# Seven half-size products in place of eight in an encoder's gated MLP

## The chip, the cores and the metric

The kernel runs on one core of one Trainium2 chip. The metric is the device time of one execution in microseconds (us), the median of three runs. Nothing of the arithmetic is done on the host; the host only lays the arrays out.

## The reference

Two layers of an encoder on 512 tokens of 1024 features, float32. Each layer mixes tokens (neighbourhood attention beside a gated linear recurrence) and then goes through a gated MLP; `x` is added to after each of the two. What matters here is the MLP:

```
h = rmsnorm(x, g_ffn[l])
u = h @ w_up[l]                                   # 1024 -> 2 x 3072
u_act, u_lin = jnp.split(u, 2, axis=-1)
u_act = depthwise_conv(u_act, conv_ffn_w[l], conv_ffn_b[l], (1, 1))
x = x + (jax.nn.gelu(u_act, approximate=True) * u_lin) @ w_down[l]
```

`rmsnorm` divides each token by its root mean square over the features and multiplies by a gain per feature. The convolution has width 3 over neighbouring tokens.

## The kernel before

Features lie on the 128 partitions, tokens along the free axis: `x` is eight tiles `x[k]` of 128 x 512. A weight matrix is cut into blocks of 128 x 128. A matrix product in float32 is done as three products of a rounded type: each operand is split into a high part (a copy rounded to `fp32r`, on ACT) and a low part (what is left, a subtraction on DVE), and `mm3` (L242) multiplies high by high, high by low and low by high into one PSUM bank. So each 128 x 128 block of weights against 512 tokens is three matmuls of 512 columns.

Weights arrive in chunks of eight blocks (128 x 1024) in the order of `weight_plan` (L57). `chunk` (L231) takes the next one; before that it has the chunks up to three ahead split (`split_to`, L190: ACT at L205, DVE at L206) and those up to six ahead loaded by SP's DMA queue (`load_to`, L170, into the two buffers of `p_raw`). Some chunks of layer 1 are split during layer 0 (`split_later`, L212, one per call, 20 in all) by POOL's DMA queue and kept in DRAM. Tile buffers come from pools with a fixed count (`p_t` 12, `p_h` 24, `p_hi` and `p_lo` 4 each); an operation that wants a buffer waits until its last user is done. The order on each engine is fixed when the kernel is built: by priority in the order of the program, with `urgent` pieces moved forward.

The MLP of a layer begins with `x` times its gain, split (`scaled_split`); the token's factor `rbf` (one over the root mean square, the same for all features) is applied after the first product, since it commutes with it. It comes from the sum of squares over the features: a matmul with ones (`columns`, L394), a power on POOL (L399), transposes (L406) and a copy (L408). The 3072 hidden features are 24 tiles `j`; each has an activation tile (block column `j` of `w_up`) and a linear tile (block column 24 + `j`), called a pair here. Pairs 0 and 1 are computed together in four PSUM banks (`gemm_group`, tile name `up`); then each `j` takes 24 matmuls for `pa` and 24 for `pl`. `mlp_tile` (L843) does the rest of a pair: `ua = pa * rbf`, the convolution in three DVE operations, Gelu on ACT, the product with `pl`, and the split of the result into `hs[j]`.

After 12 pairs (HALF) their contribution to `w_down` is computed (`dn`): four output tiles in a group of four banks, then four one after another; `summed` (L882) multiplies by `rbf` where needed and adds to `x[m]`. Two halves make a layer. At the end of the last layer `finish` (L435) does the last two output tiles in two halves of 256 tokens, so that the final norm of the first half runs beside the products of the second; `probs_of`, the attention's probability buffers (L305), serve as output buffers there.

Tokens are stored in an order that groups them by eight columns of the grid; `natural` and `by_row` are views of a tile in the order of the convolution and back.

Of the kernel before, what the change touches and what calls it, by code (L numbers as in the profile page):

```python
# [14 lines left out]
P = 128  # L15
D = 1024
# [12 lines left out]
HALF = NJ // 2  # L29
# [26 lines left out]

def weight_plan():  # L57

    plan = []
    for l in range(L):  # L60
        def pairs(w, k0, nk, ms):
            for k in range(k0, k0 + nk, 2):
                plan.append((w, l, [(k + a, m) for a in range(2) for m in ms]))

        def column(w, m):
            plan.append((w, l, [(k, m) for k in range(8)]))

        pairs("w_in", 0, 8, [12, 13, 14, 15])
        for step in MIX:
            if step[0] == "V" and int(step[1]) % 2 == 0:  # L70
                pairs("w_in", int(step[1]), 2, [8, 9, 10, 11])
            elif step[0] == "t" and step[-1] != "b":
                plan.append(("gate", l, [(int(step[1]), dg) for dg in range(4)]))
            elif step[0] in IN_TILE and step[-1] != "b":
                column("w_in", IN_TILE[step[0]] + int(step[1]))
        for m in range(0, 8, 2):
            plan.append(("w_out", l, [(a, m + b) for b in range(2) for a in range(4)]))
        pairs("w_out", 4, 4, [0, 1, 2, 3])
        for m in (4, 6):
            plan.append(("w_out", l, [(4 + a, m + b) for b in range(2) for a in range(4)]))  # L80
        for hf in range(2):
            j0 = hf * HALF
            for j in range(j0, j0 + HALF):
                if j == 0:
                    pairs("w_up", 0, 8, [0, NJ, 1, NJ + 1])
                elif j > 1:
                    column("w_up", j)
                    column("w_up", NJ + j)
            pairs("w_down", j0, HALF, [0, 1, 2, 3])
            seq = [(j0 + k, m) for m in range(4, 8) for k in range(HALF)]  # L90
            for i in range(0, len(seq), 8):
                plan.append(("w_down", l, seq[i:i + 8]))
    return plan
# [15 lines left out]
def encoder(ctx: ExitStack, tc: tile.TileContext, x_d, w_d, cols_d, bias_d, out_d):  # L109
    nc = tc.nc  # L110
    plan = weight_plan()
# [14 lines left out]
    p_raw = pool("p_raw", 2)  # L126
# [28 lines left out]
    raws, highs, lows, halves, kept = {}, {}, {}, {}, {}  # L155
# [14 lines left out]
    def load_to(n):  # L170
        while state["load"] < min(n, len(plan)):
            i = state["load"]
            if is_kept(i):
                if i > state["use"] + 3:
# [8 lines left out]
            raws[i] = p_raw.tile([P, 1024], F32, tag="raw", name=f"raw{i}")  # L183
            for n, sl in enumerate(pieces(i)):
                nc.sync.dma_start(raws[i][:, sl], w_d[i][:, sl])
                if i == n == 0:
                    nc.sync.dma_start(x[0], x_d[0])
            state["load"] += 1

    def split_to(n):  # L190
        while state["split"] < min(n, len(plan)):
            i = state["split"]
# [796 lines left out]
```

## Time and profile before

| | |
|---|---|
| median of 3 runs | 1204.91 us (1204.35 to 1204.92) |
| the profiled execution's own time | 1204.35 us |
| its span, first to last instruction | 1202.6 us |
| PE busy, matmuls | 1188.4 us, 5534 |
| DVE busy | 752.9 us |
| ACT busy | 511.7 us |
| POOL busy | 114.0 us |
| granted TensorE clock, mean | 0.996 of full |

Busy time is the union of an engine's instructions. PE's matmuls are pipelined: one lasts 0.39 us in the records while the next begins 0.23 later, so the distance between starts is what one costs. The same holds in small for DVE and ACT. L with a number is a line of the kernel; since the helper `mm3` issues the matmuls, all of them stand at L243 to L245 and are told apart by the names of their tiles.

### The profile page before, as it was taken

The numbers are of one execution on the slowest core, as the hardware profiler recorded it, in microseconds if no ns is written. First come the engines' busy times: TensorE is split into PE (matmuls) and PEld (weight loads), VectorE is DVE, ScalarE is ACT, GpSimd is POOL, SyncE is SP. The second block draws the span as 40 slices with busy tenths as digits, with TensorE's granted clock in tenths as the row PEclk, the third lists the DMA queues.
The fourth block names the chain that finished last, engine by engine and source line by source line (L and its number), as shares of the span: only waits on it lengthen the run. The fifth ranks groups of instructions, "written<-read, shape, count | busy, mean of one in ns | idle before, by whom it ended". The sixth has DMA issues, their size and how long they took to land.

```text
span 1202.6 us, 14575 instructions
## 1 busy us (share of the span) xinstructions
PE 1188.4 (99%) x5534; PEld 992.1 (83%) x5534; DVE 752.9 (63%) x1226; ACT 511.7 (43%) x753; POOL 114.0 (9%) x230
## 2 busy tenths in 40 slices
PE   9999999999999999999999999999999999999996
PEld 8878888888888888888888888888888888888886
DVE  7988967776644567653736679587555336565443
ACT  6668854434321334422408578354233213333231
POOL 1102110123210122200002012000000000000000
PEclk9999999999999999999999999999999999999998
DMA  7222214376643376733256442232323232323222
GB/s 237 82 87 89 82 38 139 106 237 236 221 164 103 134 231 215 237 115 104 88 176 200 130 159 71 62 112 90 98 96 104 90 105 88 104 89 105 88 70 70
DMA packets 51046, 151.86 MB, mean 126 GB/s; under 512 B 6432, under 2 KB 9632, under 8 KB 50976
## 3 DMA queue, kind: packets, MB, share of 16 engines
q1 hardware_dynamic: 41792, 122.21, 31.1%
q0 software_dynamic: 8640, 28.32, 7.2%
q8 instruction: 43, 0.70, 0.2%
q10 hardware_dynamic: 544, 0.40, 0.1%
q14 instruction: 27, 0.22, 0.1%
HBM read 129.93 MB, written 20.97 MB: 125 GB/s over the span
## 4 chain that ended last, share of the span: by engine, by line
PE 91%; ACT 4%; DVE 3%; issue 1%; DVEq 0%; POOLq 0%; POOL 0%; ACTq 0%
PE dn L243 7%; PE dn L245 7%; PE dn L244 7%; PE pl L243 7%; PE pa L243 7%; PE pa L244 7%; PE pl L244 7%; PE pa L245 7%; PE pl L245 7%; PE out L245 2%; PE out L243 2%; PE out L244 2%; PE s L690 1%; PE xr L243 1%; PE up L243 1%; PE xr L244 1%
## 5 line engine op out<-in xcount | busy, mean ns | idle before, releaser
L205 ACT ACTIVATE hi<-raw 128x1024 fp32r<-128x1024 f32 (+1 forms) x189 | 197.6, 1046 | 380.5 <-PE dn L244 154.3
L206 DVE TENSOR_TENSOR lo<-raw,hi 128x1024 fp32r<-128x1024 f32 (+1 forms) x189 | 227.8, 1206 | 134.7 <-ACT hi L205 133.3
L845 DVE TENSOR_TENSOR ua<-pa,g_ffn_rb 128x512 f32<-128x512 f32 x44 | 30.4, 692 | 104.5 <-PE pa L245 104.5
L853 ACT ACTIVATE uc<-uc,cols 128x512 f32<-128x512 f32 x48 | 34.8, 724 | 116.2 <-DVE uc L851 116.1
L854 DVE TENSOR_TENSOR ua<-pl,uc 128x512 f32<-128x512 f32 x44 | 30.3, 689 | 45.0 <-PE pl L245 43.4
L467 POOL TENSOR_TENSOR fin_r<-fin_ms,expo 128x2 f32<-128x2 f32 x2 | 1.4, 696 | 377.0 <-DVE fin_ms L465 377.0
L851 DVE SCALAR_TENSOR_TENSOR uc<-ua,cols,uc 128x511 f32<-128x511 f32 x48 | 36.0, 751 | 1.6
L228 POOL DMA_DIRECT2D kept<-lhi x36 | 19.5, 542 | 182.1 <-ACT lhi L222 180.2
L849 DVE SCALAR_TENSOR_TENSOR uc<-ua,cols,uc 128x511 f32<-128x511 f32 x48 | 35.8, 746 | 0.1
L705 ACT ACTIVATE prob<-prob,mx 128x192 f32<-128x192 f32 (+1 forms) x64 | 27.5, 431 | 16.1 <-DVE mx L703 16.0
L223 DVE TENSOR_TENSOR llo<-lraw,lhi 128x512 fp32r<-128x512 f32 x36 | 24.7, 688 | 13.9 <-ACT lhi L222 13.9
L818 DVE TENSOR_TENSOR dns<-dn,g_ffn_rb 128x512 f32<-128x512 f32 x24 | 16.3, 689 | 24.8 <-PE dn L245 24.8
L222 ACT ACTIVATE lhi<-lraw 128x512 fp32r<-128x512 f32 x36 | 22.1, 616 | 8.0 <-DMA lraw<-in_w 8.0
L245 PE MATMUL out<-atth,lo 128*128 128x512 f32 x64 | 25.4, 397 | 0.0
L244 PE MATMUL out<-attl,hi 128*128 128x512 f32 x64 | 25.1, 394 | 0.0
L243 PE MATMUL out<-atth,hi 128*128 128x512 f32 x64 | 24.9, 402 | 0.0
L848 DVE TENSOR_SCALAR uc<-ua,cols 128x512 f32<-128x512 f32 x48 | 23.4, 488 | 1.5
L228 POOL DMA_DIRECT2D kept<-llo x36 | 19.5, 542 | 45.9 <-DVE llo L223 42.8
L690 PE MATMUL s<-k,q_pair 128*128 128x192 f32 (+1 forms) x128 | 22.7, 317 | 0.1
L640 POOL CAST edge<-vh 64x128 fp32r<-64x128 f32 x24 | 9.5, 394 | 120.3 <-ACT vh L627 55.9
L698 DVE CUSTOM_DVE_ANT_0 prob<-s,bias 128x192 f32<-128x192 f32 (+1 forms) x64 | 18.3, 337 | 3.9 <-PE s L690 3.6
L690 PEld LDWEIGHTS s<-k,q_pair 128*128 128x128 f32 x128 | 19.8, 190 | 1.0 <-DVE k L604 0.8
(935 smaller groups left out, 3633.6 us busy)
## 6 DMA issues: line engine op xcount, KB each, us to landing
raw<-in_w SPq DMA_DIRECT2D x183, 512.0 KB, 3.5
lraw<-in_w POOLq DMA_DIRECT2D x36, 256.0 KB, 4.6
kept<-lhi POOLq DMA_DIRECT2D x36, 256.0 KB, 2.5
kept<-llo POOLq DMA_DIRECT2D x36, 256.0 KB, 3.0
hi<-kept SPq DMA_DIRECT2D x36, 256.0 KB, 2.9
lo<-kept SPq DMA_DIRECT2D x36, 256.0 KB, 4.0
x<-in_x SPq DMA_DIRECT2D x8, 256.0 KB, 4.9
bias<-in_bias SPq DMA_DIRECT2D x8, 224.0 KB, 2.5
```

What stands on the lines that cost most here:

```text
L205: nc.scalar.activation(hi[:, sl], raw[:, sl], AF.Copy)
L206: nc.vector.tensor_tensor(out=lo[:, sl], in0=raw[:, sl], in1=f32(hi[:, sl]), op=ALU.subtract)
L228: nc.gpsimd.dma_start(d, f32(parts[h][n]))
L243: nc.tensor.matmul(ps, a[0], b[0], start=start, stop=False)
L244: nc.tensor.matmul(ps, a[0], b[1], start=False, stop=False)
L245: nc.tensor.matmul(ps, a[1], b[0], start=False, stop=stop)
L690: nc.tensor.matmul(ps[:, o:o + ROWS * w], q_pair[:, b], kt[:, ROWS * kc0:ROWS * (kc0 + w)], start=True, stop=True)
L845: nc.vector.tensor_tensor(out=by_row(ua), in0=natural(pa), in1=natural(rbf[0]), op=ALU.mult)
L849: nc.vector.scalar_tensor_tensor(out=c[:, 1:], in0=ua[:, :T - 1], scalar=w[0], in1=c[:, 1:], op0=ALU.mult, op1=ALU.add)
L851: nc.vector.scalar_tensor_tensor(out=c[:, :T - 1], in0=ua[:, 1:], scalar=w[2], in1=c[:, :T - 1], op0=ALU.mult, op1=ALU.add)
L853: nc.scalar.activation(c, c, AF.Gelu_apprx_tanh, bias=col("conv_ffn_b", j, l))
L854: nc.vector.tensor_tensor(out=natural(ua), in0=natural(pl_), in1=by_row(c), op=ALU.mult)
```

## The change

The product of `w_up` with `h` is done, for pairs 3 to 23 of each layer, by one level of Strassen's algorithm in the form with few additions. The two by two scheme: rows are the two tiles of a pair (activation, linear), the contraction is cut in two halves of four blocks, the tokens in two halves of 256. Seven products of four blocks against 256 tokens take the place of eight (`turn`). The weights' operands are the plain halves (parts a and d) and sums of them (parts b and c), made by `pair_sums` on POOL and split like any weights: 3.5 chunks per pair. The seven operands on the token's side are made once a layer by `operands`, from `x` times gain times `rbf`, with differences on POOL. Three products add into the bank of product 1, from which copies are taken on the way (`u1`, `u2`, `u4`), and product 4 adds into that of product 7.

Since the operands hold `rbf` already, nothing is scaled after these products. Pairs 0 to 2 (PLAIN) stay as they were, now in six banks; the statistics come at k = 2 in place of 6. The MLP goes in four pieces of six pairs (PIECE) in place of two of 12. The first product of the convolution moves from DVE to ACT. `split_later` is called among the down products. To make room, `probs_of`, `edge` and `q_pair` are taken per layer from the new pool `p_sum`, which also holds the weights' sums, and the output buffers at the end come from it as well.

The core of the diff:

```diff
+FIRST_TURNS = [(0, 1), (0, 2), (1, 1), (0, 6), (1, 2), (0, 7), (0, 5), (1, 6), (0, 3), (1, 7), (0, 4), (1, 5)]
+TURNS = [(0, 1), (0, 2), (-1, 3), (0, 6), (0, 7), (-1, 4), (0, 5)]
+
+
+PART = {1: ("a", 0), 2: ("a", 1), 6: ("b", 0), 7: ("b", 1), 5: ("c", 0), 3: ("c", 1), 4: ("d", 0)}
+
+
+def turns(j0, j1):
+
+    seq = [(j0 + d, n) for d, n in FIRST_TURNS]
+    for j in range(j0 + 2, j1):
+        seq += [(j + d, n) for d, n in TURNS]
+    return seq, [(j1 - 1, 3), (j1 - 1, 4)]
...
-    p_raw = pool("p_raw", 2)
+    p_raw = pool("p_raw", 4)
+    p_sum = pool("p_sum", 4)
...
+    def pair_sums(i):
+
+
+        a, b = raws[i], raws[i + 1]
+        s23 = p_sum.tile([P, 1024], F32, tag="sum", name=f"sb{i}")
+        s14 = p_sum.tile([P, 1024], F32, tag="sum", name=f"sc{i}")
+        lower, upper = slice(0, 512), slice(512, 1024)
+        for out, x0, x1, op in ((s14[:, lower], b[:, lower], b[:, upper], ALU.add),
+                                (s23[:, lower], s14[:, lower], a[:, lower], ALU.subtract),
+                                (s23[:, upper], a[:, lower], b[:, lower], ALU.subtract),
+                                (s14[:, upper], a[:, upper], s23[:, lower], ALU.subtract)):
+            nc.gpsimd.tensor_tensor(out=out, in0=x0, in1=x1, op=op)
+        sums[i] = {"b": s23, "c": s14}
...
+            part = part[1] if isinstance(part[1], str) else ""
+            if part == "a":
+                pair_sums(i)
...
+            if part == "d":
+                src = raws[i + 1][:, 512:]
+                hi = big(p_fb, "fb", f"hi{i}d", F32R)
+                lo = big(p_fb, "fb", f"lo{i}d", F32R)
+                cuts = (slice(0, 512),)
+            else:
+                src = sums[i][part] if part in ("b", "c") else raws[i]
+                hi = p_hi.tile([P, 1024], F32R, tag="hi", name=f"hi{i}{part}")
+                lo = p_lo.tile([P, 1024], F32R, tag="lo", name=f"lo{i}{part}")
+                cuts = pieces(i)
...
+        def gated(j, ua, halves_of):
...
-            nc.vector.tensor_scalar(out=c, in0=ua, scalar1=w[1], scalar2=None, op0=ALU.mult)
+            nc.scalar.activation(c, ua, AF.Copy, scale=w[1])
...
-            nc.vector.tensor_tensor(out=natural(ua), in0=natural(pl_), in1=by_row(c), op=ALU.mult)
+            for n, lin in enumerate(halves_of):
+                cs = slice(n * N2, (n + 1) * N2)
+                nc.vector.tensor_tensor(out=natural(ua[:, cs]), in0=natural(lin), in1=by_row(c)[:, :, 4 * n:4 * n + 4],
+                                        op=ALU.mult)
...
+        def plain_tile(j, pa, pl_):
+
+            ua = big(p_t, "t", f"ua{l}{j}")
+            nc.vector.tensor_tensor(out=by_row(ua), in0=natural(pa), in1=natural(rbf[0]), op=ALU.mult)
+            lin = big(p_t, "t", f"lin{l}{j}")
+            nc.vector.tensor_tensor(out=lin, in0=pl_, in1=rbf[0], op=ALU.mult)
+            gated(j, ua, (lin[:, :N2], lin[:, N2:]))
+            hs[j] = plain_split(p_h, "h", ua, f"h{l}_{j}")
...
+        def operands(k):
+            def tile_of(name, dt=F32R):
+                taken[0] += 1
+                return big(p_h, "h", name, dt) if taken[0] <= 12 else big(p_xg, "xg", name, dt)
+
+            whole = big(p_t, "t", f"na{l}{k}")
+            other = big(p_t, "t", f"nb{l}{k}")
+            low, high = slice(0, N2), slice(N2, T)
+            for t, k_, src, dst in ((whole, k, low, low), (whole, k + 4, high, high),
+                                    (other, k, high, low), (other, k + 4, low, high)):
+                nc.vector.scalar_tensor_tensor(out=t[:, dst], in0=x[k_][:, src], scalar=col("g_ffn", k_, l),
+                                               in1=rbf[0][:, src], op0=ALU.mult, op1=ALU.mult)
+            s12 = big(p_t, "t", f"nc{l}{k}")
+            s34 = big(p_t, "t", f"nd{l}{k}")
+            for out, a, b in ((s12[:, low], other[:, low], whole[:, low]), (s12[:, high], whole[:, high], s12[:, low]),
+                              (s34[:, low], whole[:, high], other[:, low]), (s34[:, high], other[:, high], s12[:, high])):
+                nc.gpsimd.tensor_tensor(out=out, in0=a, in1=b, op=ALU.subtract)
+            for src, at in ((whole, (1, 3)), (s12, (5, 6)), (s34, (7, 4))):
+                hi, lo = tile_of(f"oh{l}{k}{at[0]}"), tile_of(f"ol{l}{k}{at[0]}")
+                nc.scalar.activation(hi, src, AF.Copy)
+                nc.vector.tensor_tensor(out=lo, in0=src, in1=f32(hi), op=ALU.subtract)
+                for n, cs in zip(at, (low, high)):
+                    operand[n][k] = hi[:, cs], lo[:, cs]
+                if at[0] == 1:
+                    both = tile_of(f"o{l}{k}2")
+                    nc.scalar.activation(both[:, low], other[:, high], AF.Copy)
+                    nc.vector.tensor_tensor(out=both[:, high], in0=other[:, high], in1=f32(both[:, low]), op=ALU.subtract)
+                    operand[2][k] = both[:, low], both[:, high]
...
+        def turn(j, n):
+            c, half = take_part(j, n)
+            h = held.setdefault(j, {})
+            if n in (1, 7, 2):
+                pl = {1: ps_s, 7: ps_pt, 2: ps_o}[n]
+                h["ps", n] = psum(pl, f"up{l}{j}_{n}")[:, 0:N2]
+            ps = h["ps", {1: 1, 6: 1, 5: 1, 3: 1, 7: 7, 4: 7, 2: 2}[n]]
+            for k in range(4):
+                a = [t[:, (4 * half + k) * P:(4 * half + k + 1) * P] for t in c]
+                b = operand[n][k]
+                first = k == 0 and n in (1, 7, 2)
+                mm3(ps, a, b, first, k == 3, n in (6, 5, 3, 4))
+
+            def copy(name):
+                h[name] = p_t.tile([P, N2], F32, tag="t", name=f"{name}{l}{j}")
+                with urgent():
+                    nc.scalar.activation(h[name], ps, AF.Copy)
+
+            def added(out, a, b):
+                with urgent():
+                    nc.vector.tensor_tensor(out=out, in0=a, in1=b, op=ALU.add)
+
+            if n == 1:
+                copy("u1")
+            elif n == 6:
+                copy("u2")
+            elif n == 5:
+                copy("u4")
+                h["lin"] = big(p_t, "t", f"lin{l}{j}")
+                added(h["lin"][:, N2:], h["u4"], h["ps", 7])
+            elif n == 2:
+                h["ua"] = big(p_t, "t", f"ua{l}{j}")
+                added(by_row(h["ua"])[:, :, 0:4], natural(h["u1"]), natural(ps))
+            elif n == 3:
+                with urgent():
+                    nc.scalar.activation(by_row(h["ua"])[:, :, 4:8], natural(ps), AF.Copy)
+            elif n == 4:
+                added(h["lin"][:, :N2], h["u2"], ps)
+                gated(j, h["ua"], (h["lin"][:, :N2], h["lin"][:, N2:]))
+                hs[j] = plain_split(p_h, "h", h["ua"], f"h{l}_{j}")
+                del held[j]
...
+        for j0 in range(0, NJ, PIECE):
+            last = j0 == NJ - PIECE
+            if j0 == 0:
+                banks = [psum(pl, f"up{l}{i}") for i, pl in enumerate((ps_o, ps_mm, ps_mm, ps_mm, ps_s, ps_pt))]
+                for k in range(8):
+                    if k == 2:
+                        xn2.st.columns(D, psum(ps_s, f"fcps{l}")[:, 0:4])
+                    r = xn2.split(k)
+                    c = chunk("w_up", l, (k, 0))
+                    for i in range(6):
+                        mm3(banks[i], blk(c, i), r, k == 0, k == 7)
+                    if k == 2:
+                        rbf[0] = xn2.st.rows(xn2.st.r, ps_s)
+                        for i in range(4):
+                            operands(i)
+                for j in range(PLAIN):
+                    plain_tile(j, banks[2 * j], banks[2 * j + 1])
+            seq, end = turns(max(j0, PLAIN), j0 + PIECE)
+            for j, n in seq:
+                turn(j, n)
 
             def summed(m, ps):
...
+                with urgent():
+                    nc.vector.tensor_tensor(out=x[m], in0=ps, in1=x[m], op=ALU.add)
...
+                if later:
+                    split_later()
...
+            for j, n in end:
+                take_part(j, n)
+            banks = group_banks(1, f"dn{l}{j0}")
+            for k in range(0, PIECE, 2):
+                c = chunk("w_down", l, (j0 + k, 0))
+                for a in range(2):
+                    for i in range(4):
+                        mm3(banks[i], blk(c, 4 * a + i), hs[j0 + k + a], k + a == 0, k + a == PIECE - 1)
+                    if k + a == 0:
+                        for j, n in end:
+                            turn(j, n)
+                if later:
+                    split_later()
...
         for m in (6, 7):
-            products(0, m, bank(0, m), 0, HALF)
+            products(0, m, bank(0, m), 0, PIECE)
         ps = bank(1, 6)
         products(1, 6, ps, 0, 5)
         r0 = columns(0)
-        products(1, 6, ps, 5, 9)
-        rows(0, r0)
-        products(1, 6, ps, 9, HALF)
+        products(1, 6, ps, 5, PIECE)
         for k in range(6):
             gained(k)
-        products(1, 7, bank(1, 7), 0, HALF)
+        ps = bank(1, 7)
+        products(1, 7, ps, 0, 3)
+        rows(0, r0)
+        products(1, 7, ps, 3, PIECE)
         r1 = columns(1)
```

## Rows read from the trace of the kernel before

**Rows 1.** The page: busy time of each engine, and the chain by engine.
```profile
PE 1188.4 (99%) x5534; PEld 992.1 (83%) x5534; DVE 752.9 (63%) x1226; ACT 511.7 (43%) x753; POOL 114.0 (9%) x230
...
PE 91%; ACT 4%; DVE 3%; issue 1%; DVEq 0%; POOLq 0%; POOL 0%; ACTq 0%
```

**Rows 2.** Window of layer 0's first up stage: us, busy us by engine.
```profile
238.00:336.00 98.00, 98.00 (x435) 81.16 (x434) 66.35 (x90) 40.78 (x55) 26.66 (x50) 1.00 0.69 228
```

**Rows 3.** PE's timeline: first matmuls of pairs 2 and 3 (start us, us).
```profile
227.64 0.39 PE L243 MATMUL pa<-xg_g_ffn_0h,hi 128*128 128x512 f32 x1
...
238.52 0.39 PE L243 MATMUL pa<-xg_g_ffn_0h,hi 128*128 128x512 f32 x1
```

**Rows 4.** PE's timeline: 256-column matmuls at the end, 36 apart.
```profile
1175.81 0.28 PE L244 MATMUL dnf<-h_23l,hi 128*128 128x256 f32 x1
...
1180.13 0.28 PE L244 MATMUL dnf<-h_23l,hi 128*128 128x256 f32 x1
```

**Rows 5.** Groups by form on DVE: busy us, mean ns, idle before.
```profile
L206 DVE TENSOR_TENSOR lo<-raw,hi 128x1024 fp32r<-128x1024 f32 x183 | 223.8, 1223 | 130.5 <-ACT hi L205 129.1 <-DMA lo<-kept 0.9
...
L446 DVE TENSOR_TENSOR x<-dnf,x 128x256 f32<-128x256 f32 x4 | 1.7, 423 | 6.2 <-PE dnf L245 6.2
```

**Rows 6.** DVE's timeline, four operations back to back.
```profile
206.48 1.22 DVE L206 TENSOR_TENSOR lo<-raw,hi 128x1024 fp32r<-128x1024 f32 x1
207.61 0.68 DVE L818 TENSOR_TENSOR oas<-out,att_rb 128x512 f32<-128x512 f32 x1
208.22 0.74 DVE L361 SCALAR_TENSOR_TENSOR xg_g_ffn_4l<-x,cols,xg_g_ffn_4h 128x512 fp32r<-128x512 f32 x1
208.87 0.69 DVE L387 TENSOR_TENSOR g_ffn_acc<-g_ffn_acc,g_ffn_sq 128x512 f32<-128x512 f32 x1
```

**Rows 7.** Groups by form on ACT.
```profile
L205 ACT ACTIVATE hi<-raw 128x1024 fp32r<-128x1024 f32 x183 | 193.8, 1059 | 376.9 <-PE dn L244 154.3 <-PE pa L244 139.1 <-issue 27.0
...
L448 ACT ACTIVATE finsq<-x 128x256 f32<-128x256 f32 x4 | 1.7, 417 | 15.5 <-DVE x L446 15.5
```

**Rows 8.** Groups by form on POOL.
```profile
L228 POOL DMA_DIRECT2D kept<-lhi x36 | 19.5, 542 | 182.1 <-ACT lhi L222 180.2
...
L308 POOL MEMSET prob<- 128x1024 f32 x2 | 1.9, 948 | 0.0
...
L315 POOL MEMSET q_pair<- 64x512 f32 x1 | 0.5, 520 | 0.0
```

**Rows 9.** Timelines of POOL and DVE around two casts.
```profile
649.14 1.21 DVE L581 TENSOR_TENSOR_SCAN fb<-a,ti 128x512 f32<-128x512 f32 x1
...
649.22 1.22 POOL L639 CAST edge<-vh 64x128 fp32r<-64x128 f32 x1
...
116.92 0.69 DVE L655 TENSOR_TENSOR z<-gate,g_mix_rb 128x512 f32<-128x512 f32 x1
...
117.10 0.29 POOL L640 CAST edge<-vh 64x128 fp32r<-64x128 f32 x1
```

**Rows 10.** Timelines at layer 0's entry to the MLP.
```profile
204.45 0.39 PE L243 MATMUL up<-xg_g_ffn_0h,hi 128*128 128x512 f32 x1
...
219.16 0.68 DVE L387 TENSOR_TENSOR g_ffn_acc<-g_ffn_acc,g_ffn_sq 128x512 f32<-128x512 f32 x1
...
220.77 0.95 PE L394 MATMUL fcps<-ones,g_ffn_acc 128*128 128x1 f32 x8
...
225.08 0.60 ACT L408 ACTIVATE g_ffn_rb<-g_ffn_rps 128x512 f32<-128x512 f32 x1 [3.23 <-PE g_ffn_rps L406]
```

**Rows 11.** The kernel's end: DVE's timeline, and a window.
```profile
1184.91 3.22 DVE L479 SCALAR_TENSOR_TENSOR out<-x,cols,fin_rps 128x256 f32<-128x256 f32 x8 [1.59 <-PE fin_rps L474]
...
1190.32 0.42 DVE L446 TENSOR_TENSOR x<-dnf,x 128x256 f32<-128x256 f32 x1 [0.94 <-PE dnf L245]
...
1190.00:1202.60 12.60, 1.91 (x13) 1.34 (x11) 3.00 (x5) 0.81 (x2) 0.70 (x1) 0.62 0.24 83
```

**Rows 12.** DMA issues on the page: KB each, us to landing.
```profile
raw<-in_w SPq DMA_DIRECT2D x183, 512.0 KB, 3.5
```

More of the change, by code (lines that the diff above doesn't have):

```diff
@@ L72, in weight_plan @@
             elif step[0] == "t" and step[-1] != "b":
-                plan.append(("gate", l, [(int(step[1]), dg) for dg in range(4)]))
+                add("gate", [(int(step[1]), dg) for dg in range(4)])
             elif step[0] in IN_TILE and step[-1] != "b":
@@ L110, in encoder @@
     nc = tc.nc
-    plan = weight_plan()
+    plan, units = weight_plan()
     def pool(name, bufs, space=None):
@@ L182, in load_to @@
                 continue
[L183 to L187, printed above, removed]
-            state["load"] += 1
+            for i in units[u][3]:
+                if i in raws:
+                    continue
+                raws[i] = p_raw.tile([P, 1024], F32, tag="raw", name=f"raw{i}")
+                for n, sl in enumerate(pieces(i)):
+                    nc.sync.dma_start(raws[i][:, sl], w_d[i][:, sl])
+                    if i == n == 0:
+                        nc.sync.dma_start(x[0], x_d[0])
@@ L190, in split_to @@
     def split_to(n):
-        while state["split"] < min(n, len(plan)):
-            i = state["split"]
-            if is_kept(i) and i > state["use"] + 2:
+        while state["split"] < min(n, len(units)):
+            u = state["split"]
+            what, _, part, (i, *_) = units[u]
+            if is_kept(i) and u > state["use"] + 2:
                 return
-            load_to(i + 1)
+            load_to(u + 1)
             if i in kept:
-                halves[i] = highs.pop(i), lows.pop(i)
+                halves[u] = highs.pop(i), lows.pop(i)
@@ L203, in split_to @@
             with urgent(0):
-                for sl in pieces(i):
-                    nc.scalar.activation(hi[:, sl], raw[:, sl], AF.Copy)
-                    nc.vector.tensor_tensor(out=lo[:, sl], in0=raw[:, sl], in1=f32(hi[:, sl]), op=ALU.subtract)
-            halves[i] = (hi, lo)
+                for sl in cuts:
+                    nc.scalar.activation(hi[:, sl], src[:, sl], AF.Copy)
+                    nc.vector.tensor_tensor(out=lo[:, sl], in0=src[:, sl], in1=f32(hi[:, sl]), op=ALU.subtract)
@@ L208, in split_to @@
+            halves[u] = (hi, lo)
             state["split"] += 1
@@ L438, in finish @@
         sums = {}
+        out_of = [p_sum.tile([P, 4, N], F32, tag="sum", name=f"out_of{n}") for n in range(2)]
         def products(th, m, ps, k0, k1):
@@ new lines, in layer @@
+        operand = {n: [None] * 4 for n in range(1, 8)}
+        taken = [0]
+        def operands(k):
[25 more added lines that the diff above has]
+                    operand[2][k] = both[:, low], both[:, high]
```

173 lines of the change are left out of this document (78 added, 95 removed).

## The prediction

> **What bounds the kernel now.** I read the page first: TensorE (PE) is busy for 99% of the 1202.6 us span, and 91% of the chain that ended last is matmuls [rows 1]. The windows by stage come next: in layer 0's first up stage (238 to 336 us) PE has no idle time, while VectorE (DVE) is busy 66 of 98 us, ScalarE (ACT) 41, GpSimd (POOL) 27 [rows 2]. So time goes down with PE's time per pair of tiles, as long as the others keep up; the other views price them. The sum is made against the profiled execution (1204.35 us, 1.75 around its span); the median is 0.56 above it.
>
> **PE: the term that falls.** A pair (activation tile j, linear tile j) has 2 x 8 x 3 = 48 matmuls of 512 columns. The row that begins a pair and the row that begins the next are 10.88 us apart [rows 3]: 226.7 ns each. Afterwards a pair has 7 x 4 x 3 = 84 matmuls of 256 columns. Before has such ones at the end of the kernel: 36 of them in 4.32 us, 120.0 ns each, not half of 226.7 [rows 4]; a matmul carries 13.3 ns that don't shrink with its columns. So 84 x 0.120 = 10.08 us against 10.88: 0.80 us a pair, not an eighth of 10.88 (1.36). With 21 pairs in 2 layers: 42 x 0.80 = **33.6 us** off PE. The three plain pairs and the down products keep their matmuls.
>
> The Trainium skill (TensorE: Matmul & The Clock Gate, Back-to-back issue gap) has an isolated matmul take its columns at 2.4 GHz plus 2.5 ns; by it a pair would fall from 10.36 to 9.17 us and the whole by 50 us. Rows 3 and 4 disagree by some 11 ns a matmul, and the measured spacing decides.
>
> **DVE and POOL in the up stage.** Back to back, DVE operations begin closer than their durations: a 1024-wide split subtract takes 1.22 us and the next begins 1.13 later, a 512-wide one 0.61, a 512-wide scalar_tensor_tensor 0.66 [rows 5, 6]; a 256-wide two-operand operation lasts 0.42 [rows 5], less the same 0.08: 0.34. A Strassen pair needs 3.5 units of weights split where two were (3 x 1.13 + 0.61 = 4.00), three 256-wide sums out of PSUM (1.02), two convolution taps (1.32; the first product moves to ACT), the gate in halves (0.68), the split of h (0.61): **7.63 us**, against 10.08 of PE. Before it was 5.8. The change also adds waits on PE: products 6, 5 and 3 add into the bank of product 1 and wait until ACT has copied the sum so far out of it, with the whole matmul queue behind them; two other products (2.9 us) lie between, against a copy of 0.4 and at most one weight split of 1.06 ahead of it on ACT: covered, as long as ACT isn't itself waiting for DVE. ACT's own work: 3 x 0.97 + 0.53 of weights, four 256-wide copies at 0.33, scale, Gelu and h at about 0.6 each: 6.5 us (from durations of 1.06 and 0.42 [rows 7]); not the bound.
>
> POOL gets four 512-wide two-operand sums a pair, which before has nowhere. Its memsets of 1024 and 512 give 0.836 ns an element [rows 8]. Bounds for how long one sum holds its operands: 0.43 us (one pass of 512) and 1.16 (four times the 0.29 of a 128-wide cast [rows 9]); I take two passes, 0.86. What it costs depends on DVE: a cast that normally takes 0.29 took 1.22, until the DVE scan that had started 0.08 before it ended; beside a DVE operation with one operand in PSUM it took 0.29 [rows 9]. So POOL and a DVE operation with two SBUF operands exclude each other, and 6.6 of the 7.63 us are such. Sum a pair: 7.63 + 4 x 0.86 = 11.07, less half of the 1.02 from PSUM that can run beside POOL: 10.56, **0.5 us over PE**. Two of six pairs get their sums ahead, under the down products (splits run 3 units ahead); four are left: 4 x 0.5 = 2 us a piece. Cover: the first two pairs are interleaved, so the gating starts only at the 11th product, and DVE has some 4 us spare before that. I take 0.7 us for each of the six later pieces: **4 us**. (Hold 0.43: 0. Hold 1.16: 12.27 - 10.08 = 2.2 a pair, 4 x 2.2 - 4 = 4.8 a piece, 29 us.)
>
> **The entry of the MLP, once a layer.** The operands of the seven products need the normalising row, and the first product needs operand 1 for all four k. In before the last sum of squares ends at 219.8 and the row is in SBUF at 225.7, after a wait of some 1 us for the hook at k = 6 [rows 10]; earlier hook: 224.2. PE begins the up group at 204.4 [rows 10]; 144 matmuls (three pairs, was two) and the statistics end at 238.3. Between, DVE must do 16 scalings (8 in 3.22 us [rows 11]: 0.40 each, 6.4 us), 4 + 6 splits of 512 (6.1), 3 of 256 (1.0), weights of two more k and of the first pair (0.85 x 2 + 1.13 = 2.8): 16.3 us, and POOL's twelve 256-wide differences exclude it for 12 x 0.43 = 5.2. Ready at 245.7: PE waits 7.4 us, with nothing behind it to run, since plain matmuls are over; 1 more for the banks that plain tiles 0 and 2 still hold. **8 us a layer, 16 in all.** Bounds: 2 us (POOL's differences beside no DVE work) and 15 (hold 0.58, and one pair's four sums at 1.16 in the same stretch).
>
> **Edits that come cheap, and what covers them.** The kept weights of layer 1 (20 units, each 6 POOL DMAs at 0.54 us to issue [rows 8]) move from one a pair to three or more among the down products: 11 units, 36 us of POOL in a stage of 35 us, and the next pairs' sums queue behind them on POOL. Before, one unit had 10.9 us. I take 2 us; bounds 0 and 16 (the sums of two pairs late once in each of two pieces). Raw weights: both halves of a pair stay in two of four buffers until its last part is split, so the next pair's second half is loaded at about its predecessor's start; 3.5 us to land [rows 12], three sums and a split follow, 13 of 14.4 us used: covered, and the next thing late if anything slips. Four pieces add into x 8 times each by one sum in place of two operations 16 times: even. The memsets moved into each layer: POOL is idle there. End of the kernel: products are half as long (6 for 12), so the eight scalings of the first half's output (3.2 us) come before the last sum into x instead of 2 us ahead of it [rows 11]: **2 us**, bounds 0 and 3.
>
> Sum: -33.6 + 4 + 16 + 2 + 2 = -9.6: 1194.8 for that execution, **1195** by the median.
>
> **Rivals.**
> *POOL and DVE set the pace (slower).* The exclusion holds for the whole of each sum and one lasts 1.16 us. For it: the stretched cast [rows 9]; against: casts are followed at once by DVE, whose next operation is hardly longer. Entry 15 x 2 = 30, later pieces 29, rest 4: 63 - 33.6 = +29, **1234**. Between holds of 0.86 (24 us of stalls) and 1.16 (63) the gain is used up at about 0.93 us: from there it decides. By the Trainium skill (SBUF — State Buffer, Who interferes with whom) the shared ports are an exclusive lock for the whole instruction, against a VectorE operation with two SBUF inputs when GpSimd reads SBUF; rows 9 agree, and no row shows a sum on POOL.
> *All of it hidden.* DVE takes POOL's sums into its waits, the entry is covered. For it: DVE is idle a third of the up stage [rows 2]. Only 4 us are left of the stalls: **1175**.
> *The gain is given back at the entry alone.* Gaps of 14 to 15 us a layer; PE idles, and the granted clock can fall as it does at the end (0.62 mean from 1190 on, with PE idle for most of it [rows 11]), which prices each matmul double for a while: **1204**, no change.
>
> **Chances.** Forecast 0.46 (its own range 1183 to 1202), all hidden 0.10, given back 0.07, POOL and DVE 0.37. About 0.2% is what a measurement can tell here. Faster 0.56, same 0.07, slower 0.37. The range goes from the hidden case to the slow one: 1176 to 1233.
>
> **What would show it.** PE's 256-column matmuls in the up stage start 120 ns apart, with 84 a pair; 109 or 140 would make the first term wrong. A gap of PE at each layer's first Strassen product, released by a split of an operand: 8 us expected. POOL's sums: their length, and whether DVE's two-operand splits grow beside them; over 0.93 us and DVE above 95% in the up stages is the slow rival. No gaps within pieces two to four beyond 1 us a piece. The prediction is wrong if the matmuls are not the term that falls, or if one stall outside entry and up stage is over 10 us.

## The result and the profile after

The change made the kernel slower: 1379.54 us median (1377.92 to 1382.02) against 1204.69 (1204.35 to 1204.92), four runs each, a ratio of 1.1453, 95% interval 1.1434 to 1.1473. The forecast was 1195 and the range ended at 1233. The profiled execution took 1380.2 us with a span of 1378.4.

The page of the changed kernel: busy time, the slices of PE and of its granted clock, and the chain by engine (answers to [rows 1]).

```profile
PE 1183.1 (86%) x7010; PEld 1051.9 (76%) x7010; DVE 985.3 (71%) x1464; ACT 677.9 (49%) x1089; POOL 413.7 (30%) x438
...
PE   9999998598009980699999999999589999999996
...
PEclk9999999799559995799999999999799999999998
...
PE 62%; DVE 11%; issue 8%; ACT 6%; POOL 6%; DMA 6%; POOLq 0%; DVEq 0%; ACTq 0%
```

PE was 91% of the chain and is 62%. Its busy time should have fallen by 33.6 to 1154.8 us; it is 1183.1, so 28 us of matmuls ran longer than they should, a part of them at a lower clock. Its idle time, summed over its timeline, is 187 us; before it was 5. Together: -33.6 + 28 + 182 = +176 us, and the span grew by 175.8. The slices say where: two holes in layer 0, and a dent at each layer's entry to the MLP (slices 7 to 8 and 29 to 30). The windows (stretch, its us, busy us of PE, PEld, DVE, ACT, POOL with counts, granted clock, DMA share, GB/s; answers to [rows 2]):

```profile
338.00:411.00 73.00, 3.29 (x12) 2.71 (x12) 10.91 (x14) 9.26 (x15) 26.45 (x43) 0.51 0.42 141
412.00:415.00 3.00, 3.00 (x15) 3.00 (x16) 0.56 (x2) 0.41 (x2) 0.87 (x2) 0.50 0.47 175
420.00:493.00 73.00, 70.64 (x488) 66.45 (x487) 64.42 (x73) 40.15 (x65) 31.22 (x25) 0.98 0.43 135
547.00:565.00 18.00, 0.06 (x1) 0.06 (x1) 2.43 (x4) 2.90 (x6) 4.91 (x10) 0.50 0.44 145
```

In the first and last of these stretches no engine is busy for long: in 338 to 411 POOL has the most with 26 of 73 us. That points to a chain of latencies. PE's timeline (start us, us, and in brackets the idle time before with what ended it) names its end, the same for the second hole, and the spacing in a quiet stretch (answers to [rows 3, 4]):

```profile
411.83 0.58 PE L306 MATMUL up<-oh,hi52b 128*128 128x256 f32 x1 [67.88 <-ACT u L992]
412.21 0.42 PE L307 MATMUL up<-ol,hi52b 128*128 128x256 f32 x1
412.42 0.41 PE L308 MATMUL up<-oh,lo52b 128*128 128x256 f32 x1
...
564.94 0.58 PE L306 MATMUL up<-oh,hi70b 128*128 128x256 f32 x1 [45.60 <-ACT u L992]
...
1125.69 0.28 PE L308 MATMUL up<-oh,lo166c 128*128 128x256 f32 x1
...
1128.57 0.28 PE L308 MATMUL up<-o,lo168a 128*128 128x256 f32 x1
```

The last two rows are 24 matmuls apart: 0.120 us each, as forecast. After a hole they start 0.21 us apart, at a granted clock of 0.50 (1.2 GHz) from 412 to 415. Both holes end when ACT has copied the sum so far out of the bank that product 6 adds to (u, L992). ACT's timeline shows what it did before that, and POOL's why:

```profile
349.86 0.63 ACT L283 ACTIVATE lhi<-lraw 128x512 fp32r<-128x512 f32 x1 [5.74 <-DMA lraw<-in_w]
355.52 0.63 ACT L283 ACTIVATE lhi<-lraw 128x512 fp32r<-128x512 f32 x1 [5.04 <-DMA lraw<-in_w]
...
410.87 0.63 ACT L283 ACTIVATE lhi<-lraw 128x512 fp32r<-128x512 f32 x1 [5.37 <-DMA lraw<-in_w]
411.41 0.64 ACT L992 ACTIVATE u<-up 128x256 f32<-128x256 f32 x2
```

```profile
350.78 0.54 POOL L289 DMA_DIRECT2D kept<-lhi  x1 [2.55 <-ACT lhi L283]
351.51 0.54 POOL L289 DMA_DIRECT2D kept<-llo  x1 [0.19 <-issue]
352.04 0.54 POOL L280 DMA_DIRECT2D lraw<-in_w  x1
356.45 0.54 POOL L289 DMA_DIRECT2D kept<-lhi  x1 [3.87 <-ACT lhi L283]
356.98 0.54 POOL L280 DMA_DIRECT2D lraw<-in_w  x1
357.51 0.54 POOL L289 DMA_DIRECT2D kept<-llo  x1
```

These are the kept weights, which the change moved among the down products. A half (512 wide) is loaded, rounded on ACT, subtracted on DVE and written back, and POOL issues the next load only behind the write of the high part, and at the end of a unit of two halves behind that of the low part too: some 5.5 us a half, one after the other. Eleven units are 20 halves (110 us), the nine of the next piece 16 (88 us); the down products cover the rest. PE's queue waits for ACT's copy, and the copy stands behind the last rounding in ACT's queue.

### The profile page after: what moved, and what is told of

It is laid out like the page before. It is cut to its first block, busy times and chain, and to the rows that moved or that the text cites. A ratio compares the mean times of both kernels' runs of the same rounds, so it can differ in the third digit from the quotient of the medians.

```text
span 1378.4 us, 18608 instructions
## 1 busy us (share of the span) xinstructions
PE 1183.1 (86%) x7010; PEld 1051.9 (76%) x7010; DVE 985.3 (71%) x1464; ACT 677.9 (49%) x1089; POOL 413.7 (30%) x438
## 4 chain that ended last, share of the span: by engine, by line
PE 62%; DVE 11%; issue 8%; ACT 6%; POOL 6%; DMA 6%; POOLq 0%; DVEq 0%; ACTq 0%
PE up L306 9%; PE up L307 9%; PE up L308 9%; DMA lraw<-in_w 5%; PE dn L307 4%; PE dn L306 4%; PE dn L308 4%; PE out L308 2%; PE out L306 2%; PE out L307 2%; POOL kept L289 2%; DVE ua L917 2%; PE s L756 1%; PE xr L306 1%; PE xr L307 1%
## 5 line engine op out<-in xcount | busy, mean ns | idle before, releaser
L267 DVE TENSOR_TENSOR lo<-raw,hi 128x1024 fp32r<-128x1024 f32 (+2 forms) x109 | 128.0, 1177 | 58.0 <-ACT hi L266 57.9
L266 ACT ACTIVATE hi<-raw 128x1024 fp32r<-128x1024 f32 (+2 forms) x109 | 108.8, 1001 | 95.4 <-PE up L307 33.7
L237 POOL TENSOR_TENSOR sc<-raw 128x512 f32<-128x512 f32 x42 | 59.4, 1413 | 251.0 <-DMA raw<-in_w 179.5
L237 POOL TENSOR_TENSOR sb<-sc,raw 128x512 f32<-128x512 f32 x42 | 65.6, 1562 | 51.8 <-issue 29.8
L237 POOL TENSOR_TENSOR sc<-raw,sb 128x512 f32<-128x512 f32 x42 | 74.3, 1768 | 1.8
L237 POOL TENSOR_TENSOR sb<-raw,raw 128x512 f32<-128x512 f32 x42 | 70.5, 1678 | 0.0
L992 ACT ACTIVATE u<-up 128x256 f32<-128x256 f32 x126 | 47.4, 378 | 41.8 <-PE up L308 41.8
L917 DVE TENSOR_TENSOR ua<-lin,uc 128x256 f32<-128x256 f32 x96 | 59.4, 657 | 2.9 <-ACT uc L914 2.8
L1042 DVE TENSOR_TENSOR x<-dn,x 128x512 f32<-128x512 f32 x62 | 40.9, 682 | 19.5 <-PE dn L308 19.5
L909 ACT ACTIVATE uc<-ua,cols 128x512 f32<-128x512 f32 x48 | 34.6, 721 | 5.6 <-DVE ua L925 5.2
```

Of the source, the lines that this page charges most:

```text
L237: nc.gpsimd.tensor_tensor(out=out, in0=x0, in1=x1, op=op)
L266: nc.scalar.activation(hi[:, sl], src[:, sl], AF.Copy)
L267: nc.vector.tensor_tensor(out=lo[:, sl], in0=src[:, sl], in1=f32(hi[:, sl]), op=ALU.subtract)
L917: nc.vector.tensor_tensor(out=natural(ua[:, cs]), in0=natural(lin), in1=by_row(c)[:, :, 4 * n:4 * n + 4], op=ALU.mult)
L992: nc.scalar.activation(h[name], ps, AF.Copy)
L1042: nc.vector.tensor_tensor(out=x[m], in0=ps, in1=x[m], op=ALU.add)
```

## The experiments

The theory after this reading had three parts: the burst of kept weights (most of it), POOL and DVE shutting each other out, and the operands at the entry. The rival to the first was POOL's issue time or pair sums late behind it. Times are medians; each kernel ran beside the kernel before on the same chip (1204.5 to 1204.7).

**Leave the kept weights out, after and before.** Layer 1's weights are split where they are used.

```
-        return l == 1 and (w == "gate" or w == "w_in" and bs[0][1] != 12)
+        return False
```

> The changed kernel without the kept weights: layer 1 splits all its weights itself, when it uses them. Theory (the burst): moved among the down products, each half of a kept unit takes about 5.5 us of a chain (load, ACT's high part, DVE's low part, store), some 20 and 16 halves stand in ACT's queue ahead of a copy that PE waits for, so PE idles 68 and 46 us and then runs at the low clock. Both gaps go: 1379.5 - 128 of idle time - about 25 of low clock = 1226, plus what splitting in layer 1 costs (the control run says how much). Rival (POOL's sums and DVE exclude each other and set the pace everywhere): the gaps come back at other places, over 1330.

> Control: the kernel before, also without the kept weights. What splitting those 20 units in layer 1 costs by itself. Both theories: 1205 to 1225.

Measured: 1248.61 us, and 1205.49 for the kernel before with the same edit (ratio 1.0005, 0.9993 to 1.0016). The kept weights gain the old kernel nothing that can be measured and cost the new one 131 us; both holes are gone, and PE's idle time is 64 us in place of 187.

**Spread the kept weights: at every second call, or one unit a pair and none among the down products.**

```
+                calls[0] += 1
-                if later:
+                if later and calls[0] % 2 == 0:
                     split_later()
```

The other has no call there and one a pair:

```
                 del held[j]
+                if later:
+                    split_later()
...
-                if later:
-                    split_later()
```

> The changed kernel with a kept unit at every second of the calls among the down products: 4 to 6 units a piece over four pieces in place of 11 and 9 over two. Theory (the chain of 5.5 us a half): 10 halves are 55 us against some 40 of cover, so gaps of 10 to 20 us at each of three pieces: 1226 + 30 to 60 + low clock = 1265 to 1300. Rival (only POOL's time to issue the DMAs is too much, 36 us in a stage of 35): half of it fits, no gaps, 1226 to 1235.

> The changed kernel with one kept unit after each Strassen pair, as before the change one after each pair, and none among the down products. Theory (the burst): two halves at 5.5 us a pair of 10.1 us: no long gap, at most a few us a pair where a copy waits behind a half on ACT: 1226 to 1260. Rival (the kept units' own work is too much for ACT, DVE and POOL beside Strassen's): as slow as the change, over 1340.

Measured: 1305.57 and 1307.47. The first is just above its range, the second a miss: at one unit a pair, the pace of the kernel before, it still costs 59 us over none. Its trace has many holes of 2 to 7 us, most released by the same copies (6.20 at 381, 6.78 at 498); of PE's 49 us of waiting from 300 to 660 us, 36 ended with such a copy. ACT's timeline before the first of the two:

```profile
380.41 0.63 ACT L283 ACTIVATE lhi<-lraw 128x512 fp32r<-128x512 f32 x1 [2.83 <-DMA lraw<-in_w]
380.94 0.64 ACT L992 ACTIVATE u<-up 128x256 f32<-128x256 f32 x2
```

So the length of the burst is not all of it: where such a rounding stands in ACT's queue waiting for its load, the next copy that PE needs waits too.

**Issue the loads of the kept weights one unit ahead; and pair sums and differences on DVE with the kept weights left in.**

```
-        for h in range(width(i) // 512):
...
+        if later:
+            load_later(later[0])
+        for h, raw in enumerate(ahead.pop(i)):
```

> The changed kernel, but each unit of kept weights issues the loads of the next unit before it splits its own (loads one unit ahead; POOL, ACT and DVE do the same work). Theory, a half takes 5.5 us because its load is issued only behind the write of the half before and lands 3 us later; with loads ahead a unit of two halves costs POOL's six issues of 0.54 us (3.3 us) and little more in place of 11 us: the gaps of 68 and 46 us shrink below 25 us each, 1255 to 1310 us. Rival, it is the number of splits moved and their buffers, not the landing, that fills ACT's queue: over 1340 us.

> The changed kernel with its kept weights, the differences and the pair sums on DVE instead of POOL. Theory, the burst of kept weights is a chain of its own on POOL's queue (issue the load, land, round on ACT, difference on DVE, issue the write, and only then the next load: 5.5 us a half) that holds ACT's in-order queue; the pair sums have no part in it, so only the 43 us of the exclusion go: 1325 to 1350 us, with the gaps of 68 and 46 us still there. Rival, PE waits for pair sums that stand behind the kept writes on POOL's queue: 1205 to 1240 us, both gaps gone.

Measured: 1285.58 and 1329.27, both inside the theory's ranges. Loads ahead alone give 94 us back, with the same work on each engine: the chain of latencies made most of the holes. Without any sum on POOL the holes stay, so pair sums behind the writes were not their cause. PE's timelines of the two kernels, loads ahead first:

```profile
357.23 0.58 PE L317 MATMUL up<-oh,hi52b 128*128 128x256 f32 x1 [17.80 <-ACT u L1003]
...
466.43 0.58 PE L317 MATMUL up<-oh,hi70b 128*128 128x256 f32 x1 [7.15 <-ACT u L1003]
```

```profile
397.11 0.58 PE L306 MATMUL up<-oh,hi52b 128*128 128x256 f32 x1 [62.45 <-ACT u L992]
...
541.19 0.58 PE L306 MATMUL up<-oh,hi70b 128*128 128x256 f32 x1 [41.30 <-ACT u L992]
```

**From here without kept weights (1248.6 us): the operands' differences on DVE; then the pair sums too.**

```
-                nc.gpsimd.tensor_tensor(out=out, in0=a, in1=b, op=ALU.subtract)
+                nc.vector.tensor_tensor(out=out, in0=a, in1=b, op=ALU.subtract)
...
-            nc.gpsimd.tensor_tensor(out=out, in0=x0, in1=x1, op=op)
+            nc.vector.tensor_tensor(out=out, in0=x0, in1=x1, op=op)
```

> The changed kernel with no kept weights (1248.6 us) and the 16 operand differences a layer on DVE instead of POOL. In that kernel PE idles 19 us at layer 0's entry of the MLP and 18 at layer 1's, with DVE busy back to back from 222 to 258 us and its operations at up to twice their length beside POOL. Theory, POOL and DVE exclude each other: 16 differences of 0.41 us on DVE (6.6 us) replace 16 holds of 0.72 us or more (11.5 us and more); DVE's stretch gets 0 to 6 us shorter a layer, since the pair sums on POOL still hold it: 1234 to 1249 us, the long differences on POOL (0.7 to 2.65 us) gone. Rival, DVE merely has too much of its own: 6.6 us longer a layer: 1260 to 1264 us.

> As the kernel with the differences on DVE, and the four sums a pair on DVE too: POOL does nothing big beside DVE. Theory, exclusion costs the entry and about 3 us of PE in each of the six later pieces: DVE's 512-wide gate operation is back at 0.75 us from 0.9, its 256-wide product at 0.42 from 0.74; DVE needs 7.63 + 4 x 0.61 = 10.07 us a pair beside PE's 10.08, the stalls at the pieces' starts shrink: 1220 to 1240 us. Rival, DVE is then the bound of the up stage because it also adds x and splits: 1250 to 1270 us with stalls all along the up stage.

Measured: 1236.33 and 1205.70. Giving DVE more work made the kernel 43 us faster; the second came out below its range. The cause can be read directly. DVE's and POOL's timelines of the kernel without kept weights, a quiet stretch of layer 1:

```profile
1063.36 1.60 DVE L910 SCALAR_TENSOR_TENSOR uc<-ua,cols,uc 128x511 f32<-128x511 f32 x1 [0.20 <-ACT uc L909]
1065.00 1.67 DVE L912 SCALAR_TENSOR_TENSOR uc<-ua,cols,uc 128x511 f32<-128x511 f32 x1
1066.58 2.31 DVE L267 TENSOR_TENSOR lo182c<-sc,hi182c 128x1024 fp32r<-128x1024 f32 x1
```

```profile
1063.12 1.29 POOL L237 TENSOR_TENSOR sc<-raw 128x512 f32<-128x512 f32 x1 [9.46 <-DMA raw<-in_w]
1064.37 1.74 POOL L237 TENSOR_TENSOR sb<-raw,raw 128x512 f32<-128x512 f32 x1
1066.07 1.74 POOL L237 TENSOR_TENSOR sb<-sc,raw 128x512 f32<-128x512 f32 x1
1067.89 2.16 POOL L237 TENSOR_TENSOR sc<-raw,sb 128x512 f32<-128x512 f32 x1
```

They take turns. POOL's first sum, alone, takes 1.29 us and ends at 1064.41; DVE's tap, begun inside it, ends 0.55 later at 1064.96. POOL's second ends at 1066.11, DVE's second tap 0.56 later, and the split (1.22 us when alone) 1.08 after POOL's third sum. By form, this kernel and then the one with all sums on DVE (busy us, mean ns, idle before):

```profile
L917 DVE TENSOR_TENSOR ua<-lin,uc 128x256 f32<-128x256 f32 x96 | 67.2, 740 | 0.7 <-ACT uc L914 0.6
```

```profile
L917 DVE TENSOR_TENSOR ua<-lin,uc 128x256 f32<-128x256 f32 x96 | 36.6, 419 | 0.7 <-ACT uc L914 0.7
...
L237 DVE TENSOR_TENSOR sb<-sc,raw 128x512 f32<-128x512 f32 x42 | 28.9, 687 | 0.4
```

A sum costs 0.69 us on DVE and 1.29 of both engines on POOL. By the Trainium skill (SBUF — State Buffer, Who interferes with whom) the port pair that DVE and POOL share is an exclusive lock, and a DVE instruction with two SBUF inputs contends with a POOL instruction that reads SBUF; the handovers above agree, and come instruction by instruction.

**Make a quarter of the operands: with sums on POOL, and with all on DVE.** The operands of one k serve for all four, so three quarters of that work are left out; no kept weights in either.

```
-                        for i in range(4):
-                            operands(i)
+                        operands(0)
+                        for n in range(1, 8):
+                            operand[n] = [operand[n][0]] * 4
```

> The changed kernel with no kept weights (1248.6 us) and the operands of the halves made for one of the four pairs of contraction tiles only and used for all four: it leaves three quarters of the operand work out (12 differences, 12 scaled products, 12 splits a layer and more). Theory, the making of the operands is what PE waits for at the entry of the MLP (19 us idle and some 10 us of low clock a layer): 1190 to 1205 us, the gap of 14 us in each layer gone. Rival, the gap comes from the splits of the plain group's weights and the pair sums, not from the operands: 1235 to 1249 us.

> The kernel with no kept weights and with differences and sums on DVE (1205.7 us), the operands of the halves made for one of the four pairs of contraction tiles and used for all: three quarters of the operand work left out. Theory, what is left at the entry in that kernel (8 us idle and some 7 us of low clock a layer) is the making of the operands on DVE and nothing else, and the rest of the up stage runs at PE's pace: 1172 to 1180 us, which is the time before less the 33.6 us of PE work and a few us more of idle time. Rival, a cost of the seven products that is not at the entry remains: 1185 to 1203 us.

Measured: 1209.95 and 1177.59. The first misses its range from above: POOL still costs 32 us where most of the operand work is gone. The second is inside. It is about what the seven products give if little waits: 26.9 us less than before, near the 33.6 of PE work less the 6.9 us by which its idle time (11.7) is over that of before (4.9).

**Move work at the entry: products 1 and 2 first; four plain pairs; then with two banks emptied first.** All with no kept weights and all sums on DVE. In the first, the scaled operands of all k come before any difference, and the group's weight splits are put ahead. In the second all eight banks take plain pairs, and the splits of the group's last weights are put ahead. The third empties the banks of pairs 0 and 3 first.

```
-                            operands(i)
+                            direct(i)
+                        for i in range(4):
+                            differences(i)
```

```
-PLAIN = 3
+PLAIN = 4
```

```
-                for j in range(PLAIN):
+                for j in (0, 3, 1, 2):
                     plain_tile(j, banks[2 * j], banks[2 * j + 1])
+            with urgent(j in (0, 3)):
...
```

> As the kernel with differences and sums on DVE, and two changes of order at the entry of the MLP: the plain group's weight splits come ahead of the operands on DVE, and the operands of products 1 and 2 of all four contraction tiles are made before any difference is. Theory, what counts at the entry is when the first product's operands are there, not when all are: 8 scaled pairs, 4 splits and 4 half splits are some 12 us of DVE, with the weights' splits 16, so they are there at 238 us, when the plain group ends; the 14 us gaps go, and most of the low clock behind them: 1185 to 1210 us. Rival, only the whole amount of DVE work counts (32 us from 222 us on): the gap moves behind the plain group and stays over 8 us: 1220 to 1240 us.

> The kernel with no kept weights and with differences and sums on DVE (1205.7 us), and four pairs of tiles in the plain group in place of three (all eight PSUM banks; the last bank's first four steps follow when the statistics have left it), so PE has 43.5 us of plain products beside the making of the operands instead of 32.6. Theory, at the entry DVE needs 32 us from 222 us on, to 254 us, and PE runs dry at 238: with PE's work reaching to 249 the idle 8 us and the low clock behind it (some 7 us) go in each layer, for 0.8 us more of PE work: 1174 to 1190 us. Rival, the operands' tiles come free only as the longer group ends and the first product's bank must be emptied first, so the stall moves along with the group: 1195 to 1210 us.

> The kernel with four pairs in the plain group (1208.2 us), with the emptying of the banks of plain pairs 0 and 3, which the first products need, put ahead of everything else on DVE. Theory, PE stood 6.9 us at 250 us only because the emptying of the first bank came at 256.4, last in DVE's order, though the first product's operands and weights were there at 250.5: the stall falls to some 2 us at that place and some of the 3.9 us after it, and the low clock gets shorter: 1188 to 1200 us. Rival, DVE's amount of work sets it and the stall only moves behind the first products: 1203 to 1210 us.

Measured: 1214.18, 1208.18 and 1209.81, all misses, none better than 1205.70. In each the first stall shrinks or moves and another comes: 7.74 us before product 6 in the first; 6.89 at 257 us in the second, until DVE had emptied a bank; 0.99, 1.23, 1.88 and then 6.66 at 270 in the third, where DVE is busy without a break from 240 to 270 us and the copy that ends the stall stands on ACT behind work of the plain tiles that waits for DVE. The rivals of the second and the third came true; that of the first, 1220 to 1240, was too high. None of the three helps while DVE is full.

**A whole plain piece in front.** As with all sums on DVE; pairs 0 to 5 of each layer are plain, 18 of 24 use the seven products; operands 0 are emitted ahead of pair 3, 1 behind pair 4, 2 and 3 behind pair 5.

```
-PLAIN = 3
+PLAIN = 6
...
+                operands(0)
...
+                for j in range(3, PLAIN):
...
+                    gemm_column(pa, "w_up", l, j, xg2)
+                    gemm_column(pl_, "w_up", l, NJ + j, xg2)
+                    plain_tile(j, pa, pl_)
+                    if j == 4:
+                        operands(1)
+                for i in (2, 3):
+                    operands(i)
```

> The kernel with no kept weights and with differences and sums on DVE (1205.7 us), with the whole first piece of each layer (six pairs of tiles, not three) computed plainly; the seven products are used for 18 of 24 pairs a layer, and the operands are made while PE does the plain pairs and the first piece's down products (some 60 us of PE work after the plain group). Theory, the 28 us of the entry are a matter of place: with 36 pairs at 0.8 us less PE work, 28.8 us, and the 6 us of idle time that stayed when three quarters of the operand work was left out: 1178 to 1190 us, no gap at the entry and PE's clock full. Rival, DVE has no room in the first piece either (plain tiles 29 us, operands 28, splits of weights 22, additions to x 5.5, against 98 us of PE): the stall comes back at the first product of the second piece, 1195 to 1206 us.

Measured: 1180.83 us (1180.51 to 1181.74), ratio to before 0.9804, 0.9791 to 0.9818: faster than both kernels, and than the one before by some 2%. The windows 238 to 260 us of four kernels: the changed one, all sums on DVE, a quarter of the operands, and this one (columns as above, PE first, clock third from the end).

```profile
238.00:260.00 22.00, 7.15 (x32) 5.91 (x33) 18.52 (x23) 8.27 (x13) 14.07 (x13) 0.69 0.18 56
```

```profile
238.00:260.00 22.00, 13.03 (x59) 11.17 (x58) 21.64 (x38) 10.91 (x16) 0.00 (x0) 0.69 0.24 72
```

```profile
238.00:260.00 22.00, 20.83 (x167) 20.20 (x167) 21.51 (x36) 15.83 (x25) 0.00 (x0) 1.00 0.20 70
```

```profile
238.00:260.00 22.00, 22.00 (x98) 18.21 (x97) 22.00 (x39) 13.25 (x18) 0.00 (x0) 1.00 0.24 77
```

DVE is as full in the last as in the second, 22 of 22 us, but PE has plain matmuls of its own beside it. The entry's stall was a matter of place; the price is the 0.8 us of six more plain pairs, three a layer.

## Why the prediction was wrong

The runs make a ladder. What a step is worth depends on what is gone already: moving the sums off POOL gives 50 us with the kept weights in (1379.5 to 1329.3) and 43 without.

| kernel | us | step |
|---|---|---|
| before | 1204.7 | |
| a quarter of the operands, all on DVE, no kept weights | 1177.6 | -27: PE's term and small idle times |
| all operands | 1205.7 | +28: the entry |
| sums and differences on POOL | 1248.6 | +43: POOL beside DVE |
| kept weights (the change) | 1379.5 | +131: their place and buffers |

*PE, -33.6.* Right: the matmuls start 0.120 us apart. From the gap of an isolated matmul in the Trainium skill (TensorE: Matmul & The Clock Gate, Back-to-back issue gap) they would be 0.109 apart, an estimate; the rows decide against it.

*Edits that come cheap: kept weights, taken at 2 us, bounds 0 and 16.* This step failed, by 129 us. I counted POOL's issue time (36 us in a stage of 35) and asked only who waits behind POOL, the pair sums. Two things were left out. A half is a chain, load to write to next load, of 5.5 us, so eleven units take 110 us and not 36. And its ACT and DVE parts stand in queues that run in order: the copies of PSUM that the change itself adds, and on which PE waits, came behind them. I had called those copies covered "as long as ACT isn't itself waiting for DVE"; ACT waited for a DMA.

Why the same 36 halves cost the old kernel nothing is shown in part. There POOL mostly issues the two loads of a unit back to back, and they land before ACT comes to them; in the changed kernel a write stands between any two loads. POOL's timeline of the kernel before, then the roundings on ACT, before and after (busy us, mean ns, idle before):

```profile
243.88 1.09 POOL L219 DMA_DIRECT2D lraw<-in_w  x2
```

```profile
L222 ACT ACTIVATE lhi<-lraw 128x512 fp32r<-128x512 f32 x36 | 22.1, 616 | 8.0 <-DMA lraw<-in_w 8.0
```

```profile
L283 ACT ACTIVATE lhi<-lraw 128x512 fp32r<-128x512 f32 x36 | 22.6, 629 | 150.3 <-DMA lraw<-in_w 142.3 <-issue 8.1
```

In the up stages of the old kernel PE waited for nothing on ACT. And the change has one more edit here: the halves' high and low parts come from `p_t`, which the loads and the copies of PSUM use as well, and no longer from `p_fb`. Whether that is what drove the loads apart no run tests, so place, copies and buffers share the 131 us undivided.

*DVE and POOL, taken at 4 us, upper bound 29.* The mechanism was right, the hold too small: 1.29 us where I took 0.86 and allowed 1.16. I put the point from which it decides at 0.93, so by the measured hold the slow rival was the case to forecast. Without kept weights the kernel is at 1248.6, above that rival's 1234. Of the 43 us, 32 appear with most of the operand work gone: 12 are two gaps of 0.6 and 1.4 us in each of the six later pieces, 8 more idle time at the two entries, where the clock falls to 0.50 too, and 12 more busy time of PE. The other 10.5 belong to the operands.

*Entry, taken at 16 us for both layers, bounds 4 and 30.* Mis-sized: measured 28 without POOL's part, 39 with it (1248.6 - 1210.0). DVE had more in the stretch than I listed: with everything on DVE it runs without a break from 222.0 us, and the last split that the first products wait for ends at 251.5, 29.5 us against my 21.5. Besides the differences (16, where I counted twelve) I had left out the sums of two pairs (8 x 0.61 = 4.9) and two more weight splits (2.3). The row itself came 2 us sooner than the 224.2 I put (my own terms give 224.7). Of the 28 us (30 between the profiled executions) 17 are idle time of PE, close to my 16 only by luck, since the work that they were to come from was counted too small and begins sooner. The other 13 are longer busy time, and the low clock behind the stall (0.69 over 238 to 260 us) was in a rival, not in the forecast. The stall also came earlier than said: not at the first product of halves, but inside the plain group, whose last weight split stood behind the operands on DVE, as PE's timeline of the changed kernel shows:

```profile
251.26 2.07 PE L308 MATMUL up<-xg_g_ffn_7h,lo 128*128 128x512 f32 x4 [14.06 <-DVE lo L267]
```

*End of the kernel, 2 us.* Right: the wait before the last statistics is 2.73 us and was 0.69. The kernel before, and the changed one:

```profile
1191.31 0.61 PE L463 MATMUL fin_cps<-ones,finsq 128*128 128x1 f32 x4 [0.69 <-ACT finsq L448]
```

```profile
1368.54 1.01 PE L512 MATMUL fin_cps<-ones,finsq 128*128 128x1 f32 x4 [2.73 <-ACT finsq L497]
```

The three terms that failed, 129, 39 and 12 us over what I took, make 180 of the 185 us between forecast and result. What stays open: why the loads came apart, and what the kept weights would cost in the new place with their old buffers. With loads ahead 37 us are left over the kernel without kept weights; in the profiled executions, 40 us apart, 33 are idle time of PE (97 against 64) and 7 longer busy time, and no run takes them away.

## What to carry to other kernels

When a step is moved, work out its own chain from load to next load, and list on every in-order engine that it touches what stands behind it and who waits for that; check that it keeps its buffers. A step that was free in the old place can be dear beside a new wait. Two engines that shut each other out are one resource: add their times, and where no row prices an operation on one of them, let the bound be several times the other's. The entry's stall went here when the waiting engine had three more pairs of work that it can do anyway and the operands were spread behind them; one more pair, or another order on the engine that was already full, did not cure it.

## What was unexpected of the hardware

A 512-wide sum of two SBUF operands takes POOL 1.29 us alone and DVE 0.69, and beside each other they alternate instruction by instruction, so DVE's 256-wide product went from 419 to a mean of 740 ns. After holes PE's 256-column matmuls start 0.21 us apart, not 0.12, at a granted clock of 0.50; with gaps of 4.5 us (all sums on DVE) the clock at the entry was down to 0.69 over 22 us as well, as with one of 14.
